# Issuing the modulation-weight loads for VectorE from GpSimd's queue instead of SyncE's

## Chip, cores and metric

The kernel runs on one core of one Trainium2 chip. The metric is the device time of one execution in microseconds (us). Times of runs are medians of repeated executions; the profile is one execution recorded by the hardware profiler.

## What is computed

A decoder trunk of two layers over 256 tokens of width 2048, in fp32. Each layer is attention (three groups of heads) followed by an MLP with squared ReLU; each of the two halves is wrapped in RMS norms and modulated by vectors that come from a conditioning vector `c`. Cut to what matters here:

```
def layer(x, ...):
    mod = silu(c) @ w_mod + b_mod            # 2048 x 12288 per layer
    s1, sc1, g1, s2, sc2, g2 = split(mod, 6) # shift, scale, gate, twice
    h = rms_norm(x, g_pre_mix) * (1 + sc1) + s1
    p = h @ w_in                             # 2048 x 5908
    x = x + g1 * rms_norm(mix_heads(p) @ w_out, g_post_mix)
    h = rms_norm(x, g_pre_mlp) * (1 + sc2) + s2
    u = square(relu(h @ w_up))               # 2048 x 8192
    x = x + g2 * rms_norm(u @ w_down, g_post_mlp)
```

## The kernel before

All weights come from HBM as fp32 and are used once. A matrix product is made in units of 1 MB: `unit` (L225) takes a tile `raw` of 128x4x512, loads it (L227), then in two halves ScalarE casts it to a high part `hi` (L241) and VectorE makes the rest `lo` = raw - hi (L242), and TensorE multiplies both (L259 to L261 in `gemm_b`, L287 and L289 in `chunk_a`). The tiles `raw` come from a pool of four buffers.

The product silu(c) @ w_mod has a single row, so it is mostly made by VectorE. `mod_chunk` (L121) works on 1024 columns: it loads 1 MB pieces of w_mod (L133, 128x2x1024), VectorE multiplies each row block by a column of `cact` and adds it to `acc` (L149 for the first, L151 for the others), and at the end TensorE sums over the partitions (L171, L180). For a gate the result goes to `gg` (L172, L173), which takes two small loads of 512 columns, `bb` and `gb` (L168, L169; one buffer each). Where `pe` is true, at the start of layer 0 alone, TensorE does the products in place of VectorE, on pieces of 2 MB (L142).

`mod_chunk` is a generator: `Spread.tick` pulls a piece of it after every so many weight units, so that the 176 loads of w_mod lie between those of the other weights. Where a piece lands is set by `ring`: in attention it alternates between a tile of `big` (named S in the profile) and one of the four `raw` buffers (named `rawm` there), in the MLP one in three goes to a tile X4 (X in the profile). The four `raw` buffers are so shared by `rawm`, `raw` and the compression weights `rawc`.

Every load is issued by SyncE (SP):

```
    dma = nc.sync.dma_start
```

The order of the instructions on each engine and of each queue is laid down by a scheduler when the kernel is built, and it also hands out the buffers; on the chip every queue keeps its order. SP does nothing but issue; a load waits until its buffer is free, and the loads behind it on SP wait with it.

GpSimd (POOL) computes 16 small operations, the reciprocal roots `rr` of the RMS norms in `rstd` (L293 to L295), and 4 constants at the start. They stand at the ends of the stages: the start, the boundary between attention and MLP of layer 0 (about 525 to 550 us), the one between the layers (1260 to 1285), the one in layer 1 (1690 to 1715) and the end.

Stages by time: 0 to 200 us the start and the first chunks of w_in, 200 to 450 attention of layer 0 with the rest of w_in, 450 to 525 w_out, 550 to 1260 the MLP of layer 0, 1285 to 1690 attention and w_out of layer 1, 1715 to 2418 its MLP.

Of the kernel before, what the change touches and what calls it, by code (L numbers as in the profile page):

```python
# [45 lines left out]
def trunk(ctx, tc, x, c, positions, w_mod, b_mod, g_pre_mix, g_post_mix, g_pre_mlp, g_post_mlp, w_in, b_forget,  # L46
          cmp_pe_k, cmp_pe_v, cmp_w1_k, cmp_w2_k, cmp_w1_v, cmp_w2_v, w_out, w_up, w_down, consts, out):
    nc = tc.nc
    V, A, G, T = nc.vector, nc.scalar, nc.gpsimd, nc.tensor
    dma = nc.sync.dma_start  # L50
# [11 lines left out]
    def big(tag, shape, dt=F32R):  # L62
        return bp.tile(shape, dt, tag=tag, name=tag)
# [4 lines left out]
    def ps_t():  # L68
        return pst.tile([128, 512], F32, tag="t", name="pst")
# [49 lines left out]
    def mod_chunk(l, g, q, w, pe=False, tags=None):  # L119
        kn = 2048 // w  # L120
        acc = wk.tile([128, w], F32, tag="acc" if w == 1024 else "bb", name="acc", bufs=1)  # L121
        gate = g in (2, 5)
        c0 = g * D + q * w
        have = 0
        for u in range(KT // kn):
            if have == 0:
                cyc = tags or ring[0] or (("", 1),)
                tag, have = cyc[turn[0] % len(cyc)]
                turn[0] += 1
                have = min(have, KT // kn - u)  # L130
                wide = (big(tag, [128, kn * have, w], F32) if tag else
                        rawp.tile([128, kn, w], F32, tag="raw", name="rawm"))
                dma(wide, w_mod[l, u * kn * 128:(u + have) * kn * 128, c0:c0 + w].rearrange("(k p) n -> p k n", p=128))  # L133
                u0 = u
            raw = wide[:, kn * (u - u0):kn * (u - u0 + 1)]
            have -= 1
            if pe:
                pm = ps_t()
            for k in range(kn):
                cs = cact[:, kn * u + k:kn * u + k + 1]  # L140
                if pe:
                    T.matmul(pm[32 * k:32 * k + 32], cs.to_broadcast([128, 32]), raw[:, k], start=True, stop=True,  # L142
                             tile_position=(0, 32 * k))
                elif u == 0 and k == 0:
                    with ExitStack() as es:
                        for i in hold:
                            es.enter_context(tc.issue_after(i.ins))
                        hold.clear()
                        V.tensor_scalar(acc, raw[:, k], cs, None, op0=OP.mult)  # L149
                else:  # L150
                    V.scalar_tensor_tensor(acc, raw[:, k], cs, acc, op0=OP.mult, op1=OP.add)  # L151
            if pe and u == 0:
                A.copy(acc, pm)
            elif pe:
                V.tensor_tensor(acc, pm, acc, OP.add)
            if u < KT // kn - 1:
                yield
        part = 1.0 / 32 if pe else 1.0
        if gate:
            if q == 0:  # L160
                gg_cell[0] = bp.tile([128, D], F32, tag="gg", name="gg")
            gg = gg_cell[0]
            gp = g_post_mix if g == 2 else g_post_mlp
            for i in range(w // 512):
                bb = wk.tile([128, 512], F32, tag="bb", name="bb", bufs=1)
                gb = wk.tile([128, 512], F32, tag="gb", name="gb", bufs=1)
                ci = q * w + i * 512
                dma(bb, bass.AP(tensor=b_mod.tensor, offset=b_mod.offset + (l * 6 + g) * D + ci, ap=[[0, 128], [1, 512]]))  # L168
                dma(gb, bass.AP(tensor=gp.tensor, offset=gp.offset + l * D + ci, ap=[[0, 128], [1, 512]]))  # L169
                ps = ps_t()  # L170
                T.matmul(ps, ones, acc[:, i * 512:(i + 1) * 512], start=True, stop=True)  # L171
                V.scalar_tensor_tensor(bb, ps, part, bb, op0=OP.mult, op1=OP.add)  # L172
                V.scalar_tensor_tensor(gg[:, ci:ci + 512], bb, D ** 0.5, gb, op0=OP.mult, op1=OP.mult)  # L173
        else:
            n = w // 128
            cols = slice(n * q, n * q + n)
            m = modc[:, l, {0: 0, 1: 1, 3: 2, 4: 3}[g], cols]
            ps = ps_t()
            for j in range(n):
                T.matmul(ps[:, j:j + 1], acc[:, j * 128:(j + 1) * 128], ones[:, 0:1], start=True, stop=True)  # L180
            V.scalar_tensor_tensor(m, ps[:, 0:n], part, bm[:, l, g * 16 + cols.start:g * 16 + cols.stop],
                                   op0=OP.mult, op1=OP.add)
            if g in (1, 4):
                V.scalar_tensor_tensor(m, m, 1.0, gpre[l][g // 3][:, cols], op0=OP.add, op1=OP.mult)
        yield

    def mod_groups(*lg):
        for l, g in lg:
            for q in range(2):
                yield from mod_chunk(l, g, q, 1024)  # L190
# [201 lines left out]
    for i, off in enumerate((0.25, 0.0)):  # L392
        n = st.tile([128, 2, 16], F32, tag="n", name="n", bufs=1)
# [156 lines left out]
    for l in range(DEPTH):  # L550
# [3 lines left out]
        if l == 0:  # L554
# [10 lines left out]
            def mod_first(q):  # L565
                for g in (1, 0):
                    yield from mod_chunk(0, g, q, 512, pe=g in PES, tags=(("S2", 2), ("S3", 2)))
# [172 lines left out]
        if done < 3:  # L740
            for i in range(done, 3):
                ps = chunk_b(act, W, 4876 + 344 * i, 344)
                w = 336 if i == 2 else 344
# [197 lines left out]
```

## Time and profile before

| | |
|---|---|
| median of 3 runs | 2440.83 us (2439.29 to 2443.04) |
| the profiled execution | 2435.61 us |
| its span, first to last instruction | 2433.8 us |
| mean granted TensorE clock | 0.993 |
| TensorE (PE) busy | 2364.5 us, 97% |
| VectorE (DVE) busy | 1641.5 us, 67% |
| ScalarE (ACT) busy | 1202.5 us, 49% |
| GpSimd (POOL) busy | 12.5 us, 20 instructions |
| read from HBM | 628.65 MB, 259 GB/s over the span |
| loads of w_mod | 119 rawm, 26 X, 15 S of 1 MB; 16 S of 2 MB |

SPq is SP's queue, which issues the loads; PE psg L289 means the instruction of line 289 on TensorE that writes psg. An arrow "<-" in brackets or in a list of waits names what ended the wait. In the table of stretches the columns are the length of a stretch and then the busy time and the number of instructions of each engine, the granted clock (1.00 is full), the share of the DMA engines and GB/s.

### The profile page before, as it was taken

To read this page: it belongs to the slowest core of one execution; us is meant where nothing else is said; L and a number is where in the kernel's file an instruction comes from. 1 tells how busy PE (TensorE), PEld (TensorE's weight loads), DVE (VectorE), ACT (ScalarE), POOL (GpSimd) and SP (SyncE) were. 2 spreads that over 40 slices of the span, in tenths; PEclk is the share of its full clock that TensorE was granted. 3 is DMA by queue.
4 is the path that set the end of the run, shared out by engine and by line. 5 is a ranking of instruction groups with operands and counts; after the bars stand their busy time and mean duration, and the time that the engine had idled before them with its cause. 6 is when DMAs were issued, how large, how long until landed. Compare 5 with 4: busy or idle time off the path is not lost.

```text
span 2433.8 us, 31894 instructions
## 1 busy us (share of the span) xinstructions
PE 2364.5 (97%) x12396; PEld 1964.0 (81%) x12396; DVE 1641.5 (67%) x2247; ACT 1202.5 (49%) x2001; POOL 12.5 (1%) x20
## 2 busy tenths in 40 slices
PE   5999999999999999999999999999999999999998
PEld 2678778778888888888877879888888888888887
DVE  3458678878777777777568467765755665655555
ACT  3434444455545535535545455554654553553553
POOL 0000000000000000000000000000000000000000
PEclk8999999999999999999999999999999999999999
DMA  9788988988888888888657688865666667666653
GB/s 356 285 326 298 307 300 288 351 303 292 279 310 278 309 296 286 303 283 308 202 184 280 209 282 303 282 231 186 222 225 225 225 231 231 219 203 199 189 190 121
DMA packets 292120, 632.82 MB, mean 260 GB/s; under 512 B 10609, under 2 KB 44801, under 8 KB 291713
## 3 DMA queue, kind: packets, MB, share of 16 engines
q1 hardware_dynamic: 291968, 630.79, 75.5%
q8 instruction: 97, 1.59, 0.3%
q14 instruction: 55, 0.44, 0.0%
HBM read 628.65 MB, written 2.10 MB: 259 GB/s over the span
## 4 chain that ended last, share of the span: by engine, by line
PE 90%; DVE 4%; DMA 3%; ACT 1%; issue 1%; POOL 0%; SPq 0%; DVEq 0%; POOLq 0%; ACTq 0%
PE psg L287 16%; PE psg L260 15%; PE psg L259 15%; PE psg L261 15%; PE psg L289 8%; PE psu L287 6%; PE psu L289 3%; PE psr L260 2%; PE psr L259 2%; PE psr L261 1%; PE pst L142 1%; PE pst L180 1%; DMA raw<-in_w_in_dram 1%; DMA S<-in_w_mod_dram 1%; DVE lo L242 1%; PE pst L340 1%
## 5 line engine op out<-in xcount | busy, mean ns | idle before, releaser
L242 DVE TENSOR_TENSOR lo<-raw,hi 128x1024 fp32r<-128x1024 f32 (+2 forms) x768 | 908.3, 1190 | 540.4 <-ACT hi L241 539.1
L241 ACT CAST hi<-raw 128x1024 fp32r<-128x1024 f32 (+2 forms) x768 | 781.7, 1025 | 900.3 <-PE psg L261 444.1
L259 PE MATMUL psg<-hi,S 128*128 128x512 f32 (+2 forms) x1664 | 639.8, 386 | 2.3 <-DVE S L354 1.2
L287 PE MATMUL psg<-S,hi 128*128 128x512 f32 x1792 | 640.1, 398 | 1.5 <-DVE lu L437 0.6
L260 PE MATMUL psg<-lo,S 128*128 128x512 f32 (+2 forms) x1664 | 638.0, 383 | 2.0 <-DVE lo L242 2.0
L261 PE MATMUL psg<-hi,S 128*128 128x512 f32 (+2 forms) x1664 | 636.8, 383 | 0.9 <-DVE S L355 0.9
L289 PE MATMUL psg<-S,lo 128*128 128x256 f32 x1792 | 500.8, 281 | 0.9 <-DVE lo L242 0.9
L287 PEld LDWEIGHTS psg<-S,hi 128*128 128x128 f32 x1792 | 336.9, 188 | 83.1 <-ACT hi L241 2.0
L259 PEld LDWEIGHTS psg<-hi,S 128*128 128x128 f32 x1664 | 312.1, 188 | 68.1 <-issue 4.5
L260 PEld LDWEIGHTS psg<-lo,S 128*128 128x128 f32 x1664 | 312.8, 188 | 62.1 <-DVE lo L242 3.6
L261 PEld LDWEIGHTS psg<-hi,S 128*128 128x128 f32 x1664 | 312.6, 188 | 61.4 <-DVE S L355 2.6
L289 PEld LDWEIGHTS psg<-S,lo 128*128 128x128 f32 x1792 | 338.3, 189 | 3.6 <-DVE lo L242 1.8
L151 DVE SCALAR_TENSOR_TENSOR acc<-rawm,cact,acc 128x1024 f32<-128x1024 f32 x226 | 289.3, 1280 | 26.6 <-DMA rawm<-in_w_mod_dram 24.9
L287 PE MATMUL psu<-S,hi 128*128 128x512 f32 x640 | 232.9, 398 | 0.0
L289 PE MATMUL psu<-S,lo 128*128 128x256 f32 x640 | 179.0, 280 | 0.0
L287 PEld LDWEIGHTS psu<-S,hi 128*128 128x128 f32 x640 | 120.2, 188 | 29.4 <-DVE xu L840 0.3
L289 PEld LDWEIGHTS psu<-S,lo 128*128 128x128 f32 x640 | 120.7, 189 | 0.3 <-issue 0.2
L260 PE MATMUL psr<-lo,S 128*128 128x512 f32 (+1 forms) x192 | 69.8, 363 | 1.5 <-DVE lo L242 1.5
L259 PE MATMUL psr<-hi,S 128*128 128x512 f32 (+1 forms) x192 | 68.8, 366 | 0.8 <-ACT hi L241 0.8
L261 PE MATMUL psr<-hi,S 128*128 128x512 f32 (+1 forms) x192 | 69.0, 359 | 0.0
L841 ACT ACTIVATE xu<-xu 128x256 f32<-128x256 f32 x120 | 49.3, 412 | 25.9 <-DVE xu L840 25.9
L151 DVE SCALAR_TENSOR_TENSOR acc<-X,cact,acc 128x1024 f32<-128x1024 f32 x48 | 61.4, 1280 | 0.3
(207 smaller groups left out, 1652.7 us busy)
## 6 DMA issues: line engine op xcount, KB each, us to landing
raw<-in_w_up_dram SPq DMA_DIRECT2D x128, 1024.0 KB, 5.4
raw<-in_w_down_dram SPq DMA_DIRECT2D x128, 1024.0 KB, 5.3
rawm<-in_w_mod_dram SPq DMA_DIRECT2D x119, 1024.0 KB, 6.6
raw<-in_w_in_dram SPq DMA_DIRECT2D x72, 1024.0 KB, 7.2
S<-in_w_mod_dram SPq DMA_DIRECT2D x16, 2048.0 KB, 11.1
raw<-in_w_out_dram SPq DMA_DIRECT2D x32, 1024.0 KB, 6.4
X<-in_w_mod_dram SPq DMA_DIRECT2D x26, 1024.0 KB, 7.5
raw<-in_w_in_dram SPq DMA_DIRECT2D x24, 688.0 KB, 5.5
```

Source lines behind the costliest of these rows:

```text
L142: T.matmul(pm[32 * k:32 * k + 32], cs.to_broadcast([128, 32]), raw[:, k], start=True, stop=True, tile_position=(0, 32 * k))
L151: V.scalar_tensor_tensor(acc, raw[:, k], cs, acc, op0=OP.mult, op1=OP.add)
L180: T.matmul(ps[:, j:j + 1], acc[:, j * 128:(j + 1) * 128], ones[:, 0:1], start=True, stop=True)
L241: A.copy(hi[:, :, :w], r)
L242: V.tensor_tensor(lo[:, :, :w], r, f32(hi[:, :, :w]), OP.subtract)
L259: T.matmul(ps[t][:, :w], xh, hi, start=first, stop=False)
L260: T.matmul(ps[t][:, :w], xh, lo, start=False, stop=False)
L261: T.matmul(ps[t][:, :w], xl, hi, start=False, stop=last)
L287: T.matmul(ps[d], hi[:, kk, ws], a.rearrange("p s n -> p (s n)"), start=(u == 0 and h == 0 and kk == 0), stop=False)
L289: T.matmul(ps[d][:, :256], lo[:, kk, ws], a[:, 0], start=False, stop=last)
L340: T.matmul(tp[:, j * 128:(j + 1) * 128], xt[:, t, k * 128:(k + 1) * 128], r, start=True, stop=True)
L841: A.activation(u, u, AF.Relu)
```

## The change

The loads of w_mod in `mod_chunk` are issued by GpSimd where VectorE works on them (`pe` false, 160 loads of 1 MB). The 16 loads for TensorE and all other loads of the kernel, `bb` and `gb` among them, stay with SyncE.

```diff
-                dma(wide, w_mod[l, u * kn * 128:(u + have) * kn * 128, c0:c0 + w].rearrange("(k p) n -> p k n", p=128))
+                (dma if pe else nc.gpsimd.dma_start)(wide, w_mod[l, u * kn * 128:(u + have) * kn * 128, c0:c0 + w].rearrange("(k p) n -> p k n", p=128))
```

SyncE, before, at the end of the last chunk of w_in in layer 0 (about 403 to 435 us in the profile); the numbers are those of the buffers:

```order
L133 DMA rawm_3510<-in_w_mod_dram 128x2x1024
L168 DMA bb_3514<-in_b_mod_dram 128x512
L169 DMA gb_3515<-in_g_post_mix_dram 128x512
L227 DMA raw_3530<-in_w_in_dram 128x4x512
L133 DMA rawm_3573<-in_w_mod_dram 128x2x1024
L168 DMA bb_3522<-in_b_mod_dram 128x512
L169 DMA gb_3523<-in_g_post_mix_dram 128x512
L133 DMA rawm_3620<-in_w_mod_dram 128x2x1024
L133 DMA rawm_3686<-in_w_mod_dram 128x2x1024
L133 DMA rawm_3721<-in_w_mod_dram 128x2x1024
L227 DMA raw_3736<-in_w_out_dram 128x4x512
```

SyncE, of the change, the same place:

```order
L169 DMA gb_3515<-in_g_post_mix_dram 128x512
L227 DMA raw_3376<-in_w_in_dram 128x4x512
L227 DMA raw_3422<-in_w_in_dram 128x4x512
L227 DMA raw_3468<-in_w_in_dram 128x4x512
L227 DMA raw_3530<-in_w_in_dram 128x4x512
L168 DMA bb_3522<-in_b_mod_dram 128x512
L169 DMA gb_3523<-in_g_post_mix_dram 128x512
L227 DMA raw_3736<-in_w_out_dram 128x4x512
```

Before, three loads of w_mod and one of w_out stand behind `bb_3522`. Of the change only the load of w_out does; those of w_mod stand on GpSimd's queue, which holds neither `bb` nor `gb`.

VectorE, at the same place, before and then of the change:

```order
L149 TENSOR_SCALAR acc_3572<-rawm_3573,cact_92 128x1024
L172 SCALAR_TENSOR_TENSOR bb_3522<-pst_3526,bb_3522 128x512
L151 SCALAR_TENSOR_TENSOR acc_3572<-rawm_3573,cact_92,acc_3572 128x1024
L173 SCALAR_TENSOR_TENSOR gg_3087<-bb_3522,gb_3523 128x512
L654 TENSOR_TENSOR X2_3175<-psg_3372,xe_3577 128x256
```

```order
L149 TENSOR_SCALAR acc_3572<-rawm_3573,cact_92 128x1024
L151 SCALAR_TENSOR_TENSOR acc_3572<-rawm_3573,cact_92,acc_3572 128x1024
L151 SCALAR_TENSOR_TENSOR acc_3572<-rawm_3620,cact_92,acc_3572 128x1024
L172 SCALAR_TENSOR_TENSOR bb_3522<-pst_3526,bb_3522 128x512
L654 TENSOR_TENSOR X2_3175<-psg_3372,xe_3577 128x256
```

The addition of the first row of `rawm_3620`, which stood behind the four operations of L654, now stands ahead of them and of L172.

GpSimd, at the boundary in layer 0, of the change; before, only the rows of L295 stand on this engine:

```order
L133 DMA rawm<-in_w_mod_dram 128x2x1024 x23
L295 TENSOR_TENSOR rr<-s_4368,mhalf 128x1
L295 TENSOR_TENSOR rr<-s_4386,mhalf 128x1
L133 DMA X_4779<-in_w_mod_dram 128x2x1024
L295 TENSOR_TENSOR rr<-s_4410,mhalf 128x1
L133 DMA rawm<-in_w_mod_dram 128x2x1024
L295 TENSOR_TENSOR rr<-s_4428,mhalf 128x1
```

The roots of the norms now share a queue with loads that wait for buffers.

## Rows read from the trace of the kernel before

**Rows 1.** The page, busy time, share of the span and instructions of each engine.

```profile
PE 2364.5 (97%) x12396; PEld 1964.0 (81%) x12396; DVE 1641.5 (67%) x2247; ACT 1202.5 (49%) x2001; POOL 12.5 (1%) x20
```

**Rows 2.** Busy time by stretch: length, engines, clock, DMA share, GB/s.

```profile
200.00:375.00 175.00, 164.71 (x1030) 135.82 (x1029) 139.26 (x324) 90.91 (x201) 0.00 (x0) 0.99 0.87 303
375.00:450.00 75.00, 69.41 (x373) 56.36 (x372) 67.53 (x107) 34.59 (x73) 0.00 (x0) 1.00 0.90 325
450.00:525.00 75.00, 74.18 (x344) 61.60 (x343) 61.58 (x57) 30.50 (x38) 0.00 (x0) 1.00 0.96 350
...
550.00:1260.00 710.00, 710.00 (x3621) 602.54 (x3620) 519.07 (x554) 353.28 (x522) 0.00 (x0) 1.00 0.82 282
...
1285.00:1690.00 405.00, 403.27 (x2224) 338.39 (x2224) 276.80 (x480) 203.98 (x372) 0.00 (x0) 1.00 0.77 265
...
1715.00:2418.00 703.00, 703.00 (x3535) 594.38 (x3534) 414.33 (x451) 354.46 (x525) 0.06 (x1) 1.00 0.64 207
```

**Rows 3.** Waits of SP's queue, 200 to 550 us: total, times, longest.

```profile
SPq L168 <- DVE gg L173: 14.2, 2, 9.7
```

**Rows 4.** Timeline of SP's queue, 402 to 427 us: start, length, what is issued.

```profile
402.91 0.37 SPq L227 DMA_DIRECT2D raw<-in_w_in_dram  x1
405.39 0.37 SPq L133 DMA_DIRECT2D rawm<-in_w_mod_dram  x1
...
407.66 0.38 SPq L227 DMA_DIRECT2D raw<-in_w_in_dram  x1
410.18 0.38 SPq L133 DMA_DIRECT2D rawm<-in_w_mod_dram  x1
420.25 0.34 SPq L168 DMA_DIRECT2D bb<-in_b_mod_dram  x1
...
421.16 1.73 SPq L133 DMA_DIRECT2D rawm<-in_w_mod_dram  x3
```

**Rows 5.** The chain of waits, 405 to 440 us: start, length, what.

```profile
418.80 0.70 DVE bb L172
419.53 0.70 DVE gg L173
...
421.16 7.32 DMA rawm<-in_w_mod_dram
428.64 1.14 issue
```

**Rows 6.** Timeline of PE, 427 to 433 us: idle time ahead in brackets.

```profile
427.14 0.49 PE L439 MATMUL pss<-X 128*128 128x128 f32 x2 [0.82 <-DVE X L654]
...
430.57 0.46 PE L439 MATMUL pss<-X 128*128 128x128 f32 x2 [1.41 <-DVE mx L451]
431.94 0.49 PE L441 MATMUL pss<-cst,lu 128*128 128x128 f32 x2 [0.91 <-DVE lu L437]
```

**Rows 7.** Timeline of SP's queue in the w_out stage.

```profile
473.50 0.37 SPq L133 DMA_DIRECT2D rawm<-in_w_mod_dram  x1
475.77 0.37 SPq L227 DMA_DIRECT2D raw<-in_w_out_dram  x1
...
483.07 0.37 SPq L133 DMA_DIRECT2D rawm<-in_w_mod_dram  x1
```

**Rows 8.** Loads of line L133, 375 to 450 us: time from issue to landing.

```profile
DMA to landing us min/median/max: 5.1/7.3/11.1
```

**Rows 9.** Timeline of POOL: start, length, idle time ahead.

```profile
532.42 0.55 POOL L295 TENSOR_TENSOR rr<-s,mhalf 128x1 f32<-128x1 f32 x1 [4.21 <-DVE ss L304]
538.04 1.80 POOL L295 TENSOR_TENSOR rr<-s,mhalf 128x1 f32<-128x1 f32 x1 [5.07 <-DVE s L318]
...
1269.66 0.55 POOL L295 TENSOR_TENSOR rr<-s,mhalf 128x1 f32<-128x1 f32 x1 [5.52 <-DVE s L318]
```

**Rows 10.** Timeline of DVE around 538 us.

```profile
537.88 1.22 DVE L242 TENSOR_TENSOR lo<-raw,hi 128x1024 fp32r<-128x1024 f32 x1
```

**Rows 11.** Timeline of SP's queue at the boundary between the layers.

```profile
1267.52 0.37 SPq L133 DMA_DIRECT2D S<-in_w_mod_dram  x1
```

## The prediction, made before the change was run

> **What bounds the kernel now.** I read the busy times first, then the table by stretch, then the waits of SP's queue and of TensorE, and last the timelines around the longest of them. The busy times say that TensorE works 97% of the span and POOL hardly at all [rows 1]. The table shows where the other 3% lie [rows 2]. In both MLPs TensorE is busy for the whole stretch, 710.00 of 710 us and 703.00 of 703: 1413 us in which no load, however issued, can gain anything, and in which one costs only if it comes so late that TensorE runs dry. In layer 1's attention 405 - 403.27 = 1.7 us are idle. The idle time that a load could have to do with lies in layer 0: 175 - 164.71 = 10.3 us from 200 to 375, 75 - 69.41 = 5.6 from 375 to 450, 75 - 74.18 = 0.8 in the w_out stage. That is 16.7 us, 0.7% of the kernel, and the ceiling of what the change can give there. DMA is at 0.90 and 0.96 of its time in the last two of these, so there is also something to lose in them.
>
> The one place where the order of SP's queue itself stops work is the wait for the buffer of `bb`: 14.2 us in two waits, the longest 9.7 [rows 3]. In the timeline SP issues a w_mod load at 410.18, then nothing until `bb` goes out at 420.25, and behind it three w_mod loads at once at 421.16 [rows 4]. The four loads from 402.91 to 410.18 hold the four shared buffers. A buffer turns round in some 9.6 us (the same place in the rotation issues at 473.50 and at 483.07 [rows 7]), so these buffers were free at about 412.5, 415.0, 417.3 and 419.8, and the three loads stood 9, 6 and 4 us behind an issue that had nothing to do with them. The chain of waits goes through it: `gg` frees the buffer of `bb`, SP issues, a w_mod load of 7.32 us lands, DVE goes on [rows 5].
>
> **The change, part by part.** *Removed from SP:* 160 issues of 0.37 us. SP has room between them ([rows 4, 7]: one issue every 2.3 to 2.5 us), so their time gives nothing back.
>
> *The three loads behind `bb`:* they stand on POOL's queue now and go out when their buffers are free. DVE then has its data earlier, and the additions that kept it from the softmax and from L437 come earlier too. TensorE's gaps at this place that wait for DVE are 0.82, 1.41 and 0.91 us [rows 6], 3.1 together. I take all three as gone: -3.1. What is late next is the w_out load, which still stands behind `bb`, and TensorE does not need it before the attention heads are done; I add nothing for it. The bounds of this term are 0 (DVE's order is busy with the same additions in either case, and the one of `rawm_3620` now stands ahead of L654, for which TensorE waits) and -5.6, all idle time of the stretch. The earlier half of layer 0's attention holds the other `bb` wait, 14.2 - 9.7 = 4.5 us; I see no gap of TensorE that follows it and take 0.
>
> *The price of an issue on POOL.* No row before shows a load issued there. The nearest rows are the roots on POOL, 0.55 us each when undisturbed, and 1.80 where DVE runs a `lo` of 1.22 us over the same time [rows 9, 10]; four of the sixteen are stretched, this one the most. SP needs 0.37 [rows 4]. So an issue on POOL takes 0.55 to 1.80 us if it is like such an operation: between 0.2 and 1.4 us more than on SP; call it x for each load. DVE is busy 0.8 to 0.9 of the time in these stages [rows 2], but most of a load's work is done by the DMA engines, so I take the middle, x = 0.8. Outside ends: nothing excludes that a second queue makes the loads land sooner (x below 0, by as much as a load now stands behind others in SP's queue, some 2 us of the 7.3), nor that a load is held by DVE operations one behind another (x = 2.5 for two of them, about 3 with what the first one has run).
>
> The "DVE blocks DMA" trap in the Trainium skill, SBUF — State Buffer, section on the two separate sides, speaks against the change: a load issued by GpSimd has its descriptors written there, and they are held up while DVE has the shared port, so that loads to be hidden under DVE belong on SP or ACT. The stretched roots [rows 9] agree that the two engines hold each other up, but whether issuing a load suffers too is not in any row before. The skill's DMA: Bandwidth & Descriptors, section on latency, gives the first byte as about 0.6 us by the hardware path and 1 us by GpSimd's; by it alone x would be 0.4, and the turnover term below 1.6 us by my estimate in place of 3.2.
>
> *What x does.* A buffer's turn is the landing, 7.3 us [rows 8], and some 2.3 until it is used up: 9.6 [rows 7]. From 375 to 450 there is no slack in that (the loads go out as the buffers come free, DMA 0.90), and 75 / 9.6 is about 8 turns. Half of the four buffers' turns hold a w_mod load, so the stage grows by 8 times x / 2 = 4x = +3.2 us at x = 0.8 (0.8 at x = 0.2, 5.6 at 1.4). In the w_out stage a unit is 24 products on TensorE, which at 74.18 us for 344 [rows 2] is 5.2 us; a turn of four buffers there brings two units and two w_mod loads [rows 7], so TensorE has 10.4 us of work for 9.6 of loading, 0.8 to spare, or 1.6 for each w_mod load: no cost up to x = 1.6. In the MLPs TensorE never waits [rows 2] and DVE has a quarter to two fifths of its time free: 0. From 200 to 375 the turns are the same kind, but other work (compression, rotation) sets the end of most steps; I take 0 and let the range hold it.
>
> *The roots.* Loads now stand ahead of roots on POOL. Between the layers the S load goes out at 1267.52, when TensorE has freed its tile, and the next root starts at 1269.66 [rows 9, 11]: 2.1 us for an issue that I put at 0.37 + 0.8. At the other boundaries the loads have more room. Cost 0 up to x = 1.8.
>
> **The sum:** -3.1 + 3.2 + 0 + 0 = +0.1 us. Against the profiled execution, 2435.61 us with a span of 2433.8, that is 2435.7. That execution is 5.2 us under the median of the runs, 2440.83, so for a median I say 2440.9, rounded 2441. With the term's own bounds the sum goes from -3.1 + 0.8 = -2.3 to 0 + 5.6 = +5.6.
>
> **Rivals.** *Faster: two queues relieve layer 0.* Weight loads no longer stand behind w_mod loads in one queue, and the wait for `bb` stops only weights. For it: the DMA is 0.87 to 0.96 busy there and landing takes 7.3 us where the smallest is 5.1 [rows 8]. Against it: the same bytes go through the same DMA engines, and much of the idle time is softmax chains. If half of the 16.7 us of idle time goes, the time is 2440.8 - 8 = about 2433. *Slower: DVE holds up POOL.* If a load is held by two or three DVE operations in a row, x is 3 in place of 0.8. Then the turnover costs 4 times 3 = 12, the gain of 3.1 stays at best, the S load delays a root by about 1 us, and the w_out stage begins to lack data: 2440.8 + 12 - 3 + 1 = 2451, or 2454 without the gain; at x = 4 and without the gain it is 2457. It decides from 4x - 3.1 = 4.9, that is x = 2.0. For it: POOL's stretched roots and a DVE that is busy 0.9 of the time from 375 to 450. Against it: a root was never held longer than one DVE operation. *The change does not do what it says:* the loads leave SP, but on POOL they stand behind one another for their buffers as they did on SP, and the `bb` wait turns out hidden. Then the sum is x alone, 2441 to 2446 for x of 0.2 to 1.4: mostly within no change.
>
> **How the numbers follow.** About 0.2%, 4.9 us, is what a measurement of this kernel can tell from no change. No measurable change: 0.41, from my sum with its bounds and most of the last rival. Faster by more: 0.27, the relief of two queues, which has the more ways to work since each microsecond earlier in layer 0 has idle time to go into. Slower by more: 0.32, the hold of POOL by DVE, and a reordering by the scheduler that falls badly (the order of DVE differs at the place shown, and in layer 1's attention). The single number is 2441. The range goes from 2430, two thirds of the idle time of layer 0 gone (-11), to 2457, the hold at x = 4 (+16); outside it I leave 0.1 at either end.
>
> **What would show it.** Right: SP shows no gap of 10 us near 410 that holds up w_mod; the three loads go out on POOL 3 us or more apart, ahead of `bb`; the issue of a load on POOL takes about 1.2 us; the PE gaps at 427 to 432 are gone and others, after landings that come later, have taken their place; the stretches of the MLPs keep 710 and 703 us. Wrong on the fast side: the idle time of TensorE from 200 to 450 falls by over 5 us. Wrong on the slow side: POOL's queue shows loads of 3 us and more, landings of w_mod over 10 us in the median, TensorE waiting for DVE's `lo` or `acc` in the w_out stage, or gaps in an MLP; any gap in an MLP would mean that x is far above my bounds, since a load there has slack of several microseconds.

## The result and the profile after

The change made the kernel slower: 2508.94 us (median of 4 runs, 2505.54 to 2515.80) against 2441.39 before, a ratio of 1.0281 with a 95% interval of 1.0255 to 1.0307, or +67.5 us. The forecast was 2441, the range ended at 2457. The profiled execution took 2511.89 us with a span of 2510.0, against 2433.8 before.

The page, busy times, then the kinds of DMA queue:

```profile
PE 2397.2 (96%) x12396; PEld 1983.1 (79%) x12396; DVE 1639.5 (65%) x2247; ACT 1203.1 (48%) x2001; POOL 129.9 (5%) x180
...
q1 hardware_dynamic: 248448, 463.01, 54.6%
q0 software_dynamic: 43520, 167.78, 18.9%
```

The change does what it says: 167.78 MB, the 160 loads, go through a queue of POOL's own. TensorE does the same 12396 products and is busy 2397.2 - 2364.5 [rows 1] = 32.7 us longer. So of the 76.2 us by which the span grew, 32.7 are longer work of TensorE on the same products and 43.5 are waits.

Busy time by stretch, the columns and stretches of [rows 2]:

```profile
200.00:375.00 175.00, 160.28 (x979) 130.47 (x978) 131.18 (x306) 86.39 (x193) 15.04 (x21) 0.96 0.79 271
375.00:450.00 75.00, 65.05 (x333) 52.80 (x332) 58.85 (x91) 28.70 (x59) 7.88 (x11) 0.93 0.83 294
...
550.00:1260.00 710.00, 682.44 (x3452) 574.43 (x3451) 500.04 (x551) 345.20 (x535) 49.22 (x66) 0.98 0.78 270
...
1285.00:1690.00 405.00, 388.98 (x2154) 327.04 (x2152) 274.92 (x495) 205.29 (x397) 26.37 (x36) 0.98 0.73 249
```

The surprise is the third row. In the MLP of layer 0 TensorE had been busy 710.00 of 710 us [rows 2]; now it is idle for 27.6 of them, at a granted clock of 0.98. (The stretches are those of the kernel before. The changed kernel is late, so its first 20 us there still belong to the boundary; from 575 to 1250 us, inside the MLP of both, the idle time is 24.6 us.) To see where the time went I compared the starts of the same `lo` operations in the two traces: the changed kernel is 20 us behind where the MLP of layer 0 begins, 59 where it ends, 74 where the attention and w_out of layer 1 end, and 75 from there on. So some 23 us are lost from 200 to 550 us, 39 in the MLP of layer 0, 14.5 from there to the end of layer 1's attention, and next to nothing in the MLP of layer 1. (The table under experiment 2 has these figures.)

Waits of DVE, 550 to 1260 us, first of the kernel before, then of the changed one (total, times, longest):

```profile
DVE acc L151 <- DMA rawm<-in_w_mod_dram: 20.0, 18, 3.2
```

```profile
DVE acc L151 <- DMA rawm<-in_w_mod_dram: 111.4, 31, 8.4
```

The longest of them, in the timelines of DVE and of TensorE:

```profile
688.14 3.49 DVE L242 TENSOR_TENSOR lo<-raw,hi 128x1024 fp32r<-128x1024 f32 x3
700.00 1.28 DVE L151 SCALAR_TENSOR_TENSOR acc<-rawm,cact,acc 128x1024 f32<-128x1024 f32 x1 [8.38 <-DMA rawm<-in_w_mod_dram]
701.20 1.22 DVE L242 TENSOR_TENSOR lo<-raw,hi 128x1024 fp32r<-128x1024 f32 x1
```

```profile
697.87 0.39 PE L259 MATMUL psg<-hi,S 128*128 128x512 f32 x1
702.48 0.79 PE L260 MATMUL psg<-lo,S 128*128 128x512 f32 x1 [4.22 <-DVE lo L242]
703.07 0.63 PE L261 MATMUL psg<-hi,S 128*128 128x512 f32 x1
703.50 0.63 PE L259 MATMUL psg<-hi,S 128*128 128x512 f32 x1
...
708.55 0.39 PE L259 MATMUL psg<-hi,S 128*128 128x512 f32 x1
```

DVE stands for 8.38 us at an addition whose w_mod piece has not landed. A `lo` stands behind that addition on DVE, and TensorE waits 4.22 us for it. Here is the same place on DVE in the order of the built programs, before:

```
L242 TENSOR_TENSOR lo_5540<-raw_5533,hi_5539 128x1024
L242 TENSOR_TENSOR lo_5574<-raw_5571,hi_5573 128x1024
L151 SCALAR_TENSOR_TENSOR acc_5306<-rawm_5639,cact_92,acc_5306 128x1024
```

and of the change:

```
L242 TENSOR_TENSOR lo_5540<-raw_5533,hi_5539 128x1024
L151 SCALAR_TENSOR_TENSOR acc_5306<-rawm_5639,cact_92,acc_5306 128x1024
L242 TENSOR_TENSOR lo_5574<-raw_5571,hi_5573 128x1024
```

The scheduler has put the addition one `lo` earlier. DVE reaches it before its data, and the `lo` that TensorE needs next, which could have been made meanwhile, waits behind it. Counted over the program: in the MLP of layer 0 the first addition of 20 of the 43 rawm pieces stands one or two `lo` operations earlier than before, 2 later; in the attention and w_out of layer 1 13 of 27 earlier; in the MLP of layer 1 none of 11. The count goes with the loss; whether it is the cause, experiments 4 and 5 test.

The `lo` operations are less than half of what TensorE waits for in this MLP. Its busy time and its longest waits in the changed kernel, 575 to 1250 us:

```profile
575.00:1250.00 675.00, 650.37 (x3285) 548.11 (x3284) 473.13 (x509) 319.78 (x477) 43.74 (x61) 0.98 0.79 274
```

```profile
PE psg L260 <- DVE lo L242: 8.5, 6, 4.2
PE psu L287 <- DVE xu L840: 8.0, 3, 4.6
PE psg L287 <- DVE xu L840: 5.6, 3, 3.0
```

Of 675 - 650.37 = 24.6 us of idle time, 13.6 end with `xu` of L840, where DVE adds the two halves of a product with w_up. It stands behind additions just as `lo` does: of the 64 pieces that DVE works on in this MLP (43 in `rawm`, 21 in X), five have their first addition one or two `xu` earlier than before, and three of the four gaps behind `xu` of over 1 us follow such an addition.

A gap also costs after it ends. In the rows of TensorE around 702 us the products are 0.43 us apart from 703.07 on and 0.23 before and after; by stretch:

```profile
690.00:697.00 7.00, 7.00 (x33) 5.79 (x32) 1.63 (x2) 2.82 (x3) 0.48 (x1) 1.00 0.99 346
...
702.00:708.50 6.50, 6.02 (x14) 4.76 (x15) 6.46 (x7) 0.93 (x1) 0.71 (x1) 0.50 0.58 192
708.50:714.00 5.50, 5.50 (x25) 4.52 (x25) 3.40 (x3) 1.64 (x3) 0.71 (x1) 1.00 1.01 358
```

After 4.22 us without a product the granted clock is 0.50 (1.2 GHz in place of 2.4) for about 6 us, and 14 products take as long as some 26 would. Over the whole trace the granted clock is 0.50 for 35.7 us before and for 90.2 us in the changed kernel, and TensorE is busy in 19.7 and 69.7 us of them. At half the clock half of that is what the clock costs: 9.9 and 34.9 us, or 25 of the 32.7 us. What the other 8 us are is not shown.

POOL itself does little wrong. Timeline of POOL and, from the same trace, time to landing of the loads of L133 from 550 to 1260 us:

```profile
709.95 0.71 POOL L133 DMA_DIRECT2D rawm<-in_w_mod_dram  x1 [1.56 <-DVE lo L242]
```

```profile
DMA to landing us min/median/max: 5.4/7.4/10.1
```

An issue takes 0.72 us in place of 0.37; it begins a median 0.41 us after its buffer is free (0.03 on SP), by the starts of the loads and the ends of the last reads; the landing, counted from the start of the issue, takes 7.4 us in the median against 7.1 before. But the 0.3 us go with the order and not with the queue. Time to landing in the same window, in experiment 1 below (POOL, old order) and in experiment 2 (SP, new order):

```profile
DMA to landing us min/median/max: 5.2/7.0/9.6
```

```profile
DMA to landing us min/median/max: 4.8/7.4/10.6
```

By the medians the price x of a load on POOL is so the later start alone, about 0.4 us, half of the 0.8 that I had taken; the shortest landing is 0.4 us longer on POOL (5.2 against 4.8 before).

### The profile page after: what moved, and what is told of

The parts are those of the page before. It is cut to its first block, busy times and chain, and to the rows that moved or that the text cites. A ratio compares the mean times of both kernels' runs of the same rounds, so it can differ in the third digit from the quotient of the medians.

```text
span 2510.0 us, 32040 instructions
## 1 busy us (share of the span) xinstructions
PE 2397.2 (96%) x12396; PEld 1983.1 (79%) x12396; DVE 1639.5 (65%) x2247; ACT 1203.1 (48%) x2001; POOL 129.9 (5%) x180
## 3 DMA queue, kind: packets, MB, share of 16 engines
q0 software_dynamic: 43520, 167.78, 18.9%
## 4 chain that ended last, share of the span: by engine, by line
PE 59%; issue 13%; DMA 11%; DVE 5%; ACT 2%; POOL 1%; POOLq 0%; DVEq 0%; ACTq 0%; SPq 0%
PE psg L287 12%; PE psg L260 10%; PE psg L259 10%; PE psg L261 10%; PE psg L289 6%; DMA rawm<-in_w_mod_dram 4%; PE psu L287 4%; DMA raw<-in_w_in_dram 2%; PE psu L289 2%; DVE acc L151 2%; DVE lo L242 1%; DMA raw<-in_w_out_dram 1%; DMA S<-in_w_mod_dram 1%; DMA raw<-in_w_down_dram 1%; ACT hi L241 1%
## 5 line engine op out<-in xcount | busy, mean ns | idle before, releaser
L242 DVE TENSOR_TENSOR lo<-raw,hi 128x1024 fp32r<-128x1024 f32 (+2 forms) x768 | 906.1, 1190 | 518.3 <-ACT hi L241 516.6
L287 PE MATMUL psg<-S,hi 128*128 128x512 f32 x1792 | 650.0, 403 | 12.8 <-DVE xu L840 5.6
L289 PE MATMUL psg<-S,lo 128*128 128x256 f32 x1792 | 506.8, 284 | 2.6 <-DVE lo L242 2.5
L151 DVE SCALAR_TENSOR_TENSOR acc<-rawm,cact,acc 128x1024 f32<-128x1024 f32 x226 | 289.5, 1281 | 145.0 <-DMA rawm<-in_w_mod_dram 143.0
L260 PEld LDWEIGHTS psg<-lo,S 128*128 128x128 f32 x1664 | 315.4, 190 | 75.5 <-DVE lo L242 17.1
L133 POOL DMA_DIRECT2D rawm<-in_w_mod_dram x119 | 85.6, 719 | 1524.1 <-DVE lo L242 712.9
L259 PE MATMUL psr<-hi,S 128*128 128x512 f32 (+1 forms) x192 | 69.7, 365 | 0.8 <-ACT hi L241 0.8
```

Source lines behind the costliest of these rows:

```text
L133: (dma if pe else nc.gpsimd.dma_start)(wide, w_mod[l, u * kn * 128:(u + have) * kn * 128, c0:c0 + w].rearrange("(k p) n -> p k n", p=128))
L242: V.tensor_tensor(lo[:, :, :w], r, f32(hi[:, :, :w]), OP.subtract)
L259: T.matmul(ps[t][:, :w], xh, hi, start=first, stop=False)
L260: T.matmul(ps[t][:, :w], xh, lo, start=False, stop=False)
L287: T.matmul(ps[d], hi[:, kk, ws], a.rearrange("p s n -> p (s n)"), start=(u == 0 and h == 0 and kk == 0), stop=False)
L289: T.matmul(ps[d][:, :256], lo[:, kk, ws], a[:, 0], start=False, stop=last)
```

## The experiments

Two theories. *Order:* with the loads on POOL the scheduler lays out another order, in which DVE meets additions before their data. *Queue:* issue on POOL is late, and the loads wait behind one another there. To separate them I took the order of each engine's instructions from the one built program and pinned it in the kernel that issues from the other queue. The loads of w_mod and the other loads were pinned each among themselves.

### 1 and 2: the queue without the order, the order without the queue

```diff
+    traced = [i for i in nc.cur_bb.bb.instructions if type(i).__name__ != "BassTilePoolBoundary"]
+    at, behind = -1, None
+    for step in ORDER:
+        if step == 30000:
+            at, behind = -1, None
+            continue
+        at += step
+        if behind is not None:
+            tc.add_manual_dep(traced[at], behind.name, mybir.DependencyInfo(
+                mybir.DependencyClass.NoSync, mybir.DependencyReason.DATA), reason="order")
+        behind = traced[at]
```

ORDER is the table of one program's order. Experiment 1 is the changed kernel with the order of before, experiment 2 the kernel before with that of the change.

> The 160 loads of w_mod are issued by POOL as in the change, but the order of all instructions on PE, DVE and ACT, of the other loads on SP and of the w_mod loads among themselves is pinned to that of the kernel before. Order theory (the loss comes from the scheduler, which with the loads on POOL puts some additions on the w_mod rows one or two lo operations earlier on DVE, so that DVE waits for their data): 2441 to 2453 us, TensorE idle in the MLP of layer 0 under 4 us, granted clock there 1.00. Queue theory (the loss comes from POOL itself: an issue of 0.72 us, a start 0.4 us after the buffer is free, the w_mod loads behind one another): 2490 us or more, DVE's waits for w_mod rows in the MLP of layer 0 near the 111 us of the change.

> All loads are issued by SP as before, but the order on PE, DVE and ACT, of the other loads and of the w_mod loads among themselves is pinned to that of the changed kernel. Order theory: 2480 to 2510 us, with TensorE gaps behind DVE's waits for w_mod rows in the MLP of layer 0 and no loss in the MLP of layer 1. Queue theory: within 8 us of 2441.

Experiment 1: 2454.28 us, ratio 1.0052 (1.0032 to 1.0071). Experiment 2: 2505.89 us, ratio 1.0263 (1.0245 to 1.0280), nearly all of the loss, with every load on SP. In waits of DVE from 575 to 1250 us, of experiment 1 and then of experiment 2 (the additions are L217 and L218 in these files):

```profile
DVE acc L217 <- DMA rawm<-in_w_mod_dram: 26.6, 22, 2.6
```

```profile
DVE acc L218 <- DMA rawm<-in_w_mod_dram: 91.8, 29, 6.0
```

and TensorE by stretch in the same window, in the same order:

```profile
575.00:1250.00 675.00, 675.00 (x3459) 573.12 (x3458) 494.14 (x527) 337.62 (x499) 43.07 (x60) 1.00 0.82 284
```

```profile
575.00:1250.00 675.00, 660.08 (x3375) 556.56 (x3375) 488.78 (x537) 332.44 (x514) 1.81 (x2) 0.99 0.80 280
```

With the old order TensorE does not wait in that MLP although POOL issues 60 loads there; with the new one it waits although SP issues them. The order theory holds: the changed kernel and experiment 1 differ in the order alone, and 2508.94 - 2454.28 = 54.7 us lie between them. A part of the queue theory is left: +14 us in experiment 1, just above the 2453 that the order theory allowed. The start of the same `lo` operations against the kernel before, in single profiled executions (us behind):

| | at 200 us | 550 | 1250 | 1650 | 2400 |
|---|---|---|---|---|---|
| changed kernel | -2.8 | 20.2 | 59.2 | 73.7 | 75.5 |
| 1: POOL, old order | -0.1 | 10.4 | 11.0 | 15.0 | 16.8 |
| 2: SP, new order | 13.8 | 36.8 | 58.9 | 72.2 | 73.8 |
| 4: POOL, old places of the additions | -1.1 | 13.0 | 21.5 | 38.8 | 39.2 |
| 5: SP, new places of the additions | 1.3 | 30.6 | 34.4 | 40.6 | 40.8 |
| 6: SP, bb later | -1.8 | 2.7 | 3.9 | 3.1 | 4.7 |
| 7: POOL, old order, later start | 0.4 | 16.1 | 22.4 | 38.3 | 39.8 |

(The profiled execution of before is 5 us under its median, so a few microseconds in a row are no effect, as row 6 shows.) In the MLP of layer 0, from 550 to 1250, the queue alone costs 0.6 us, the order alone 22.1, both 39.0: they do not add. One part of row 2 is its own: SP's mix of w_mod and other loads was left to the scheduler, and that kernel loses 13.8 us in the first 200, where the changed one loses nothing. So its near agreement with the changed kernel in total is partly chance. In the built orders 33 of the 45 w_mod loads of layer 0's attention stand one to four other loads later on SP than before, but in the MLP of layer 0 56 of 64 stand where they stood. So the 22.1 us of that MLP belong to the order of the engines; what experiment 2 loses ahead of 550 us may come from SP's mix, and no run separates the two.

### 3: the other way to free the w_mod loads

```diff
-                dma(bb, bass.AP(
+                nc.gpsimd.dma_start(bb, bass.AP(
...
-                dma(gb, bass.AP(
+                nc.gpsimd.dma_start(gb, bass.AP(
```

> Only the small loads bb and gb go to POOL, all w_mod loads stay on SP: SP's wait of 9.7 us for the buffer of bb is gone by another way, and DVE's order hardly moves. If that wait held up TensorE as the prediction's term says: 2436 to 2440 us, the TensorE gaps at 427 to 432 us gone. If it was covered: 2441 us within 3.

2453.81 us, ratio 1.0058 (1.0040 to 1.0077): slower, which neither case expected. SP's wait was gone, but the gap on TensorE at this place grew. Timeline of TensorE:

```profile
432.88 0.76 PE L439 MATMUL pss<-X 128*128 128x128 f32 x2 [3.81 <-DVE mx L451]
```

The chain of waits shows the load of `gb` ahead of it, and behind that DVE's L173 and L654:

```profile
424.22 6.83 DMA gb<-in_g_post_mix_dram
...
431.16 0.69 DVE gg L173
431.85 0.33 DVE X L654
```

A second gap of 3.1 us, at 1975 in the MLP of layer 1, has the same form: `bb` goes out on POOL when L173 has freed its buffer, and DVE waits 4.01 us for it at L172 with the work for TensorE behind. So in this kernel DVE waits for `bb` and `gb`, not for the loads that they held up. Its order was the scheduler's own again (58 instructions moved on DVE), so how much is POOL and how much the order stays open.

### 4 and 5: only the places of the additions

Pinned are only the operations of L242, L149 and L151 among each other, in experiment 4 to the order of before with the loads on POOL, in experiment 5 to the order of the change with all on SP.

```diff
+                        mine.append(V.tensor_scalar(acc, raw[:, k], cs, None, op0=OP.mult))
...
+    line = [marks[i // 2][i % 2] for i in ORDER]
+    for i, j in zip(line, line[1:]):
+        tc.add_manual_dep(j.ins, i.ins.name, mybir.DependencyInfo(mybir.DependencyClass.NoSync,
+                                                                  mybir.DependencyReason.DATA), reason="order")
```

> Loads of w_mod on POOL; pinned to the order of before are only the lo operations (L242) and the additions of w_mod rows (L149, L151) among each other on DVE; all else is the scheduler's. If the places of the additions among the lo operations are what counts: 2445 to 2460 us, near the 2454 of the first experiment, and DVE's waits for w_mod rows in the MLP of layer 0 under 40 us. If it is the rest of the order (softmax, rotation, PE): 2480 us or more.

> All loads on SP; pinned to the order of the changed kernel are only the lo operations and the additions of w_mod rows among each other. If these places count: 2470 to 2510 us, with 70 us or more of DVE waits for w_mod rows in the MLP of layer 0. If it is the rest of the order: within 8 us of 2441.

Experiment 4: 2470.77 us, ratio 1.0125 (1.0104 to 1.0147), between the two cases. With the additions put back, 38 of the 67.5 us are gone. In the table, 30.5 of the 39.0 us of the MLP of layer 0 are gone (8.5 left), DVE's waits there are 50.8 us in place of 111.4, and most of what stays lies in the two attention stages, where the rest of the order is still new. In layer 1's nothing is gained: 17.3 us from 1250 to 1650 where the changed kernel loses 14.5. So the 13 additions that moved there are not shown to be its cause. Experiment 5: 2475.81 us, ratio 1.0138 (1.0115 to 1.0161): with the new places and SP's queue 34 to 36 us are lost. Its waits of DVE from 575 to 1250 us:

```profile
DVE acc L183 <- DMA rawm<-in_w_mod_dram: 76.8, 26, 5.8
```

But only 4 us of its loss lie in the MLP, so the waits of 76.8 us were mostly covered there, and 29 lie between 200 and 550. The pin was against `lo` alone: in this program's built order no addition of the MLP stands ahead of more `xu` than before, and TensorE waits 0.8 us for `xu` there, in experiment 2 8.9 us. That fits the 4 us, but no run moves the places against `xu` by themselves. Nor are the 29 us the places alone: the scheduler laid out the rest anew, and 28 of the 45 w_mod loads of layer 0's attention stand later on SP than before. So the places against `lo` and `xu` are shown for the MLP of layer 0, by experiment 4 with the loads on POOL; which moves make up the loss in the attention stages was not tried one by one.

### 6: the wait for bb by itself

All orders pinned to those of before, but two of the w_mod loads that stood behind `bb_3522` and `gb_3523` on SP go ahead of them.

```diff
 DMA rawm_3573
-DMA bb_3522
-DMA gb_3523
 DMA rawm_3620
 DMA rawm_3686
+DMA bb_3522
+DMA gb_3523
 DMA rawm_3721
```

> Kernel before with all its orders pinned, but on SP the one pair bb, gb of layer 0 that waited 9.7 us stands behind two of the three w_mod loads that it held up; nothing else differs. If the prediction's term of -3.1 us is right, 2437 to 2438.5 us and the three TensorE gaps from 427 to 432 us gone. If the wait was covered: 2441 within 2 us, the gaps still there in sum.

2441.23 us against 2439.63, ratio 1.0005 (0.9994 to 1.0016): no change that can be told, and a gain of 3.1 us lies outside the interval, which ends at -1.5. The timeline of SP and then of TensorE, where the three gaps are those of [rows 6]:

```profile
409.74 6.41 SPq L198 DMA_DIRECT2D rawm<-in_w_mod_dram  x3
419.81 0.34 SPq L233 DMA_DIRECT2D bb<-in_b_mod_dram  x1
```

```profile
428.39 0.49 PE L504 MATMUL pss<-X 128*128 128x128 f32 x2 [2.50 <-DVE X L719]
431.98 0.70 PE L504 MATMUL pss<-X 128*128 128x128 f32 x2 [0.40 <-DVE mx L516]
433.35 0.49 PE L506 MATMUL pss<-cst,lu 128*128 128x128 f32 x2 [0.68 <-DVE lu L502]
```

The two loads were out by 416.15 (the three issues from 409.74 on) where they had waited until 421.16 and after, and the gaps are 3.6 us in sum where they were 3.1. But they are not the same gaps. The two after the late loads fell from 1.41 and 0.91 us to 0.40 and 0.68, and the one ahead of them rose from 0.82 to 2.50, because DVE now waits for `bb`. DVE in the kernel before, then in this one, then in the changed kernel, at L172 (here L237) and, before, at the first addition of a late load:

```profile
423.56 0.69 DVE L172 SCALAR_TENSOR_TENSOR bb<-pst,bb 128x512 f32<-128x512 f32 x1 [0.40 <-DMA bb<-in_b_mod_dram]
...
428.58 1.28 DVE L151 SCALAR_TENSOR_TENSOR acc<-rawm,cact,acc 128x1024 f32<-128x1024 f32 x1 [0.51 <-DMA rawm<-in_w_mod_dram]
```

```profile
425.51 0.69 DVE L237 SCALAR_TENSOR_TENSOR bb<-pst,bb 128x512 f32<-128x512 f32 x1 [2.79 <-DMA bb<-in_b_mod_dram]
```

```profile
439.81 0.69 DVE L172 SCALAR_TENSOR_TENSOR bb<-pst,bb 128x512 f32<-128x512 f32 x1 [3.36 <-DMA bb<-in_b_mod_dram]
```

With the w_mod loads ahead of it `bb` lands 5.6 us after its issue here and 6.6 in the changed kernel, where it took 3.2 before. So this run doesn't show the wait on SP to be covered; it shows that letting the loads go first moves the wait to `bb`, with nothing gained.

### 7: a later start

Experiment 1 with one more operation on POOL ahead of each load, into the tile that the load fills.

```diff
+                if not pe:
+                    extra.add(G.memset(wide[:, 0, :512], 0.0).ins.name)
                 (dma if pe else nc.gpsimd.dma_start)(wide, ...)
```

> As the first experiment (w_mod loads on POOL, all orders pinned to those of before), with a memset by POOL of 128x512 into each of the 160 tiles just ahead of its load; it waits for the buffer as the load does, so that each load starts later by the memset and its semaphore, an estimated 0.5 to 1.5 us. Nothing else differs. If a later start costs what the prediction's turnover term says (8 turns times half of the delay from 375 to 450, less around it, nothing in the MLPs), 2458 to 2468 us, the growth all ahead of 550 us and in the attention of layer 1, the MLP of layer 0 unchanged. If the MLP of layer 0 has no slack for DVE's waits even in the old order, 2475 us or more, with DVE's waits for w_mod rows there over 60 us and gaps on TensorE.

2472.31 us, ratio 1.0124 (1.0101 to 1.0147), 18 us more than experiment 1, for a start that the trace shows later by 0.58 us (a median 0.99 us after the buffer is free, 0.41 in experiment 1). For 14 of the 160 loads, 9 of them ahead of the MLP of layer 0, a memset or load of another tile stands in between, so that these can start later still. DVE is not slowed by the memsets: it is busy 1641.6 us, 1642.2 in experiment 1. POOL's timeline, and the waits of DVE from 575 to 1290 us (the additions are L220):

```profile
604.72 0.53 POOL L201 MEMSET rawm<- 128x512 f32 x1 [0.61 <-DVE lo L311]
605.65 0.71 POOL L202 DMA_DIRECT2D rawm<-in_w_mod_dram  x1 [0.41 <-POOL rawm L201]
```

```profile
DVE acc L220 <- DMA rawm<-in_w_mod_dram: 62.7, 30, 5.7
```

It falls between the two cases. The MLP of layer 0 does not break, but it costs 6.3 us in place of 0.6: the old order was near the edge there, too. The larger part, 5.7 us up to 550 and 11.9 from 1250 to 1650 over experiment 1, lies in the attention stages.

## Why the prediction was wrong

**The step that failed** is one short line: "In the MLPs TensorE never waits [rows 2] and DVE has a quarter to two fifths of its time free: 0." It took the order on DVE as given and asked only what a later load costs in it. But the scheduler makes a new order, and the built program showed that before any run. I used the built order for one place of layer 0's attention and named layer 1's, and let the additions that had changed places with `lo` operations in the MLP go. There the order alone cost 22 us and order and queue together 39 (the table, experiment 2 and the changed kernel), the queue alone 0.6. The free time of DVE was no cover: DVE keeps its order, so a wait at an addition delays the `lo` or `xu` behind it, however idle DVE is on average. A share of busy time says nothing on which operation stands ahead of which. The trace of before had a sign of it: in that MLP DVE already waited 20.0 us, in 18 waits, for w_mod pieces, and no work for TensorE came late by it. So a load there had no "slack of several microseconds", and the gaps came without an x above the bounds. The same step failed in the attention stages, at 23 and 14.5 us for the whole change, but which moves did it there stays open.

**The turnover term** was right in kind, too high in its price and far too narrow in place. The price x is about 0.4 us by the medians above, 0.8 was taken. Experiment 1 has the queue with nothing else and costs 14 us where I had 3.2. From 375 to 450 it loses about 3, but by x = 0.4 the term would give 1.6; and it loses 4 from 200 to 375, some 4 from 450 to 550 and 4 in layer 1's attention, where I had put 0. Its factor of 4 us for each microsecond of x is the part that was mis-sized: 14 us for 0.38 us in experiment 1 and 18 more for 0.58 in experiment 7 are 37 and 31.

**The gain of 3.1 us** does not exist. I had read the chain of waits as if the late load [rows 5] caused the gaps [rows 6]. But the first gap ends at 427.14, and the load lands at 421.16 + 7.32 = 428.48. DVE then waited 0.51 us for it (the row under experiment 6), and the rest of what kept DVE from the softmax was the additions' own time, 1.28 us each. And where the loads do go ahead, `bb` comes later: in experiment 6 with nothing gained, and in the changed kernel, where the loads left ahead of `bb` as forecast, with a gap of 2.79 us on TensorE in place of 0.82.

**The rivals.** The slower one named DVE holding POOL as mechanism. It did not happen: all 160 issues took 0.71 to 1.01 us, most of them 0.72, with DVE busy beside them. The trap that the Trainium skill describes (SBUF — State Buffer, on the two separate sides) would have shown as issues or landings longer by the DVE operation that holds the port. No row here shows that for a load: the longest landing of w_mod in the MLP of layer 0 is 10.1 us where it was 10.0. The first bytes that the Trainium skill gives (DMA: Bandwidth & Descriptors, on latency), 0.6 and 1 us, differ by 0.4 us; the trace has 0.4 us in the shortest landing, nothing in the median, and 0.38 in the start. The words "a reordering by the scheduler that falls badly" stood among the chances for slower, but with no price, and the range's end at 2457 came from the hold on POOL. **The clock** was no part of the prediction: about 25 of the 76 us are what products at the lower clock cost.

**What held:** the boundaries (their gaps in experiment 1 are 1.6, 3.2, 2.4 and 2.2 us, against 1.6, 3.1, 2.0 and 2.2), the MLP of layer 1, and that the change does move the queue.

## What to carry to other kernels

Where a scheduler makes the order, a change of the issuing queue is also a change of every engine's order: compare the built orders over the whole program before costing the queue, and price each operation that now stands ahead of work for the busiest engine by when its data lands. To tell the two apart, pin the order of one program in the other: here the queue alone cost 14 us and the new order 55 on top of it. A load that stands late in a queue is worth moving only if what waits for its data is late too, and if nothing that must land sooner then falls behind it.

## What the runs showed of the hardware that was not expected

A root on POOL beside loads was stretched more than any before: 2.93 us against 1.80 [rows 9].

```profile
555.25 0.73 POOL L133 DMA_DIRECT2D X<-in_w_mod_dram  x1 [2.96 <-PE psg L261]
557.38 2.93 POOL L295 TENSOR_TENSOR rr<-s,mhalf 128x1 f32<-128x1 f32 x1 [1.39 <-DVE s L318]
```

A gap of 4.22 us on TensorE was followed by about 6 us at half the granted clock, so that it cost some 3 us more than it lasted. A small load behind 1 MB loads landed late: `bb` took 5.6 and 6.6 us with w_mod loads issued just ahead of it, 3.2 without (experiment 6). And a start of loads later by 0.58 us (experiment 7) cost 18 us over 160 loads, in a kernel whose most used engine is busy 97% of the time.
